# Reading a projection's 512 columns in pieces of 32: another order for TensorE's moving operand and its sums

## The chip, the core and the metric

One core of a Trainium2 chip runs the whole program in one launch. The metric is the device time of that launch in microseconds (us); three runs of the kernel before gave 1434.5, 1430.88 and 1432.8 us, median 1432.8. The profile was taken on one further execution.

## The reference, cut to what matters

One pre-norm residual layer on x (1 x 256 x 2048, float32), then a final RMSNorm. The combined input projection is the larger part of the work:

```python
h = _rms_norm(x, norm_g)
u = jnp.einsum('bsd,dn->bsn', h, w_in)            # 256 x 2048 times 2048 x 22672
a_in, b_in, b_gate, c_qkv, c_f, c_gate, d_in, d_gate, m_logit = _split(u, IN_SIZES)
# four mixers: gated short convolution, RWKV-7 recurrence, forgetting attention, causal pooling
proj = jnp.einsum('bskc,kcd->bskd', ys, w_branch)  # four times 256 x 1024 times 1024 x 2048
gates = jax.nn.sigmoid(m_logit.reshape(bsz, s, N_BRANCH, d) + b_merge)
merged = jnp.sum(gates * proj, axis=2)
return x + jnp.einsum('bsd,de->bse', merged, w_out)  # 256 x 2048 times 2048 x 2048
```

## The kernel before, in words

The 256 tokens are two row blocks of 128. Every large projection is a *chunk* of 512 output columns (`chunk`): its weights come from HBM two rows-of-128 at a time (512 KB in `raw`, three buffers, on SP's queue), and each 128 x 512 tile is split into two fp32r parts, a high one by ScalarE (`wh`, L267, six buffers) and a low one by VectorE (`wl`, L268, six buffers). The activations are split once into high and low parts (`xh`, `xl` for the input projection; `yah` to `ydl` for the branches; `mh`, `ml` for the output). `products` (L236 to L242) then issues three matmuls for each tile and row block: high x high (L240), high x low (L241), low x high (L242). In each, the activations are the stationary operand (128 x 128, loaded into the array by a weight load of its own, PEld), and the weights' part is the moving operand: its 512 columns are streamed, and 512 sums of each of the 128 rows are added into one PSUM tile `psm` (128 x 512 f32). A chunk of the input or output projection has 16 tiles, so 96 such matmuls; one of the branch projections has 8, so 48.

Two chunks are only 328 columns wide (`b_inputs`, half 1). The last chunk of the output projection puts all its split weights into the space of earlier tiles (`keep`) and runs row block 0 first, then row block 1 from the same parts; no weight is split in that second pass.

The order is fixed before the run: a scheduler places the instructions of each engine by the priorities of `level`. The weights' split has the first claim, then the RWKV block, then attention, then the rest. In the first 740 us the projections of the mixers are interleaved on PE with the many small matmuls of RWKV (the solver of L489 and L491 is a chain on VectorE) and of attention; from there on come the pooling branch, then 16 pairs of a gate chunk and a branch chunk, and the output projection, almost all of it chunks.

Where tiles lie: in the built program every tile that a chunk's matmul reads (`wh`, `wl`, `xh`, `xl`, `yah` to `ydl`, `yb`, `yc`, `ml1`) starts at an address, in bytes of its partition, that leaves 96 when divided by 512. 512 bytes are 128 columns of float32, and 128 bytes are one piece of 32 columns.

Of the kernel before, what the change touches and what calls it, by code (L numbers as in the profile page):

```python
# [9 lines left out]
F32 = mybir.dt.float32  # L10
F32R = mybir.dt.float32r
I32 = mybir.dt.int32
AF = mybir.ActivationFunctionType
# [4 lines left out]
P = 128  # L18
T = 256
NB = 2  # L20
D = 2048
W = 1024
CH = 512
HALF = 512
KG = 2
# [69 lines left out]
def kernel(  # L95
# [29 lines left out]
    sc = nc.scalar  # L125
# [6 lines left out]
    w_br_v = [w_branch[0, n].rearrange("(k p) n -> p k n", p=P) for n in range(4)]  # L132


    pers = ctx.enter_context(tc.tile_pool(name="pers", bufs=1))
    wpool = ctx.enter_context(tc.tile_pool(name="wpool", bufs=1))
    bc_pool = ctx.enter_context(tc.tile_pool(name="bc", bufs=2))
    ynat = ctx.enter_context(tc.tile_pool(name="ynat", bufs=1))
    wk = ctx.enter_context(tc.tile_pool(name="wk", bufs=1))
    ps_main = ctx.enter_context(tc.tile_pool(name="ps_main", bufs=3, space=PSUM))  # L140
# [2 lines left out]
    def psum_ex(tag, shape=(P, 512)):  # L143
        return ps_ex.tile(list(shape), F32, name="ps_" + tag, tag=tag, bufs=1 if tag == "z" else 2)
# [7 lines left out]
    @contextmanager  # L152
    def level(n):
        own, tc.cur_priority = tc.cur_priority, at[n]
        yield
        at[n], tc.cur_priority = tc.cur_priority, own


    rstd = pers.tile([P, NB], F32, name="rstd")
    nrstd8 = pers.tile([P, NB], F32, name="nrstd8")  # L160
    ngT = pers.tile([P, D // P], F32, name="ngT")
    ones1 = pers.tile([P, 1], F32, name="ones1")
    cq = pers.tile([P, NB, 16], F32, name="cq")
    fss = pers.tile([P, NB, 4], F32, name="fss")
    frs = pers.tile([P, NB], F32, name="frs")
    fa = pers.tile([P, NB, 16], F32, name="fa")
    xh = pers.tile([P, D // P, T], F32R, name="xh")
    xl = pers.tile([P, D // P, T], F32R, name="xl")
    cst = pers.tile([P, N_CONST], F32, name="cst")

    def load_constants(lo, hi):
        nc.sync.dma_start(out=cst[:, lo:hi], in_=consts[:, lo:hi])

    def K(name):
        lo, hi = _COFF[name]
        return cst[:, lo:hi]
# [3 lines left out]
    def bcast(src, n=CH, pool=bc_pool):  # L180

        t = pool.tile([P, n], F32, name="row", bufs=2)
        gp.dma_start(out=t, in_=src.unsqueeze(0).to_broadcast([P, n]))  # L183
        return t

    def mid(t):
        return t.unsqueeze(1).to_broadcast([P, NB, t.shape[-1]])
# [45 lines left out]
        v.tensor_scalar(out=nrstd8, in0=rstd, scalar1=-float(H) ** -0.5, scalar2=None, op0=ALU.mult)  # L233


    def products(ps, sth, stl, wh, wl, k, nk, n, b):  # L236
        cols = slice(b * P, (b + 1) * P)
        o = ps[b][:, :n]
        h, l = wh[:, :n], wl[:, :n]
        nc.tensor.matmul(o, lhsT=sth[:, k, cols], rhs=h, start=k == 0, stop=False)  # L240
        nc.tensor.matmul(o, lhsT=sth[:, k, cols], rhs=l, start=False, stop=False)  # L241
        nc.tensor.matmul(o, lhsT=stl[:, k, cols], rhs=h, start=False, stop=k == nk - 1)  # L242

    def new_ps():
        return [ps_main.tile([P, CH], F32, name="psm", tag="psm") for b in range(NB)]

    def chunk(ranges, nk, sth, stl, before=lambda g: None, keep=None):


        ps = new_ps()  # L250
        n = sum(r[2] for r in ranges)
        for g in range(nk // KG):
            wh, wl = [], []
            with level(WEIGHTS):
                before(g)
                raw = wpool.tile([P, KG, CH], F32, name="raw", bufs=3)
                at = 0
                for wv, c0, w in ranges:
                    nc.sync.dma_start(out=raw[:, :, at:at + w], in_=wv[:, g * KG:(g + 1) * KG, c0:c0 + w])
                    at += w  # L260
                for j in range(KG):
                    if keep:
                        h, l = keep(g * KG + j)
                    else:
                        h = wpool.tile([P, CH], F32R, name="wh", bufs=6)
                        l = wpool.tile([P, CH], F32R, name="wl", bufs=6)
                    sc.activation(out=h[:, :n], in_=raw[:, j, :n], func=AF.Copy)  # L267
                    v.tensor_tensor(out=l[:, :n], in0=raw[:, j, :n], in1=h[:, :n].bitcast(F32), op=ALU.subtract)  # L268
                    wh.append(h)
                    wl.append(l)  # L270
            for b in range(1 if keep else NB):
                for j in range(KG):
                    products(ps, sth, stl, wh[j], wl[j], g * KG + j, nk, n, b)
        if keep:
            for k in range(nk):
                products(ps, sth, stl, *keep(k), k, nk, n, 1)
        return ps

    def chunk_in(c0, n=CH, before=lambda g: None):
        return chunk([(w_in_v, c0, n)], D // P, xh, xl, before)  # L280
# [22 lines left out]
    def shift(dst, src, n):  # L303

        gp.memset(dst[0:n, 0, :], 0.0)
        gp.dma_start(out=dst[n:112 + n], in_=src[0:112])
        gp.dma_start(out=dst[112 + n:P], in_=src[112:P - n])
        gp.dma_start(out=dst[0:n, 1, :], in_=src[P - n:P, 0, :])
# [279 lines left out]
    def lora_and_forget(lu, cf):  # L588
        lp = wk.tile([P, NB, P], F32, name="qk", bufs=2)
        shift(lp, lu, 1)  # L590
        mub = bcast(rwkv_mu[0, 3072:3200], 128)
        v.tensor_tensor(out=lp, in0=lp, in1=lu, op=ALU.subtract)
        v.tensor_tensor(out=lp, in0=lp, in1=mid(mub), op=ALU.mult)
        v.tensor_tensor(out=lu, in0=lu, in1=lp, op=ALU.add)
        sc.activation(out=lu[:, :, 0:64], in_=lu[:, :, 0:64], func=AF.Tanh)
        tp = psum_ex("r")
        for b in range(NB):
            nc.tensor.transpose(tp[:, b * P:(b + 1) * P], lu[:, b, :], ident)

        for j, (own, other) in enumerate(((lo, hi), (hi, lo))):  # L600
            sc.activation(out=loraT[own, j, :], in_=tp[own, 0:T], func=AF.Copy)
            v.tensor_tensor(out=loraT[other, j, :], in0=tp[own, 0:T], in1=loraT[own, j, :].bitcast(F32),
                            op=ALU.subtract)


        bfb = bcast(fox_bf[0], 16)
        v.tensor_tensor(out=cf, in0=cf, in1=mid(bfb), op=ALU.add)
        sc.activation(out=fa, in_=cf, func=AF.Abs)
        sc.activation(out=fa, in_=fa, func=AF.Exp, scale=-1.0)
        sc.activation(out=fa, in_=fa, func=AF.Ln, bias=ones1)  # L610
        v.tensor_scalar(out=cf, in0=cf, scalar1=0.0, scalar2=None, op0=ALU.min)
        v.tensor_tensor(out=cf, in0=cf, in1=fa, op=ALU.subtract)
        tp = psum_ex("c")
        nc.tensor.matmul(tp[:, 0:16], lhsT=K("tri"), rhs=cf[:, 0, :], start=True, stop=True)
        v.tensor_copy(out=cq[:, 0, :], in_=tp[:, 0:16])
        tp = psum_ex("c")
        nc.tensor.matmul(tp[:, 0:16], lhsT=K("tri"), rhs=cf[:, 1, :], start=True, stop=False)
        nc.tensor.matmul(tp[:, 0:16], lhsT=K("ones"), rhs=cf[:, 0, :], start=False, stop=True)
        v.tensor_copy(out=cq[:, 1, :], in_=tp[:, 0:16])
# [165 lines left out]
    for hf in range(2):  # L785
# [4 lines left out]
        for g2 in range(2):  # L790
            g = hf * 2 + g2
# [25 lines left out]
    for dc in range(4):  # L817
        mg = wk.tile([P, NB, CH], F32, name="va")
        for n, nm in enumerate("abcd"):
            gt = gate_tile(dc, n)  # L820
            ps = chunk([(w_br_v[n], dc * CH, CH)], W // P, *yT[nm])
            for b in range(NB):
                if n == 0:
                    v.tensor_tensor(out=mg[:, b, :], in0=ps[b], in1=gt[:, b, :], op=ALU.mult)
                else:
                    v.tensor_tensor(out=gt[:, b, :], in0=ps[b], in1=gt[:, b, :], op=ALU.mult)
                    v.tensor_tensor(out=mg[:, b, :], in0=mg[:, b, :], in1=gt[:, b, :], op=ALU.add)
        split_T([mh[dc // 2], ml[dc // 2]], (dc % 2) * 4, mg, 4)
# [18 lines left out]
    def keep(k):  # L847
        if k < 8:
            return spare[0][:, k, :], spare[1][:, k, :]
        i = 2 + 2 * ((k - 8) // 4)  # L850
        return spare[i][:, k % 4, :], spare[i + 1][:, k % 4, :]

    for dc in range(4):
        fg = bcast(final_g[dc * CH:(dc + 1) * CH])
        ps = chunk([(w_out_v, dc * CH, CH)], D // P, Parts(mh), Parts(ml), keep=keep if dc == 3 else None)
# [53 lines left out]
```

## Time and profile before

| what | value |
|---|---|
| three runs | 1430.88, 1432.8, 1434.5 us |
| the profiled execution's own time | 1433.31 us |
| its span in the trace | 1431.5 us (1.8 us lie outside it) |
| mean granted TensorE clock | 0.994 |
| PE, PEld, DVE, ACT busy | 98%, 80%, 69%, 51% of the span |
| HBM read | 257.44 MB, 181 GB/s over the span |

A matmul's record is longer than the distance to the next one, since matmuls are pipelined: a busy PE says only that something was in the array. What one costs is read from the distance of starts. The chain of waits is followed back from the last instruction, and its shares tell which work the end depends on.

### The profile page before, as it was taken

Reading aid. Unit: us, or ns where it says so; the run is one execution under the profiler, and the core shown is the slowest. Engines: PE = TensorE matmul, PEld = TensorE weight load, DVE = VectorE, ACT = ScalarE, POOL = GpSimd, SP = SyncE. Lnnn points to the kernel's source line nnn. Section 1 sums busy time; section 2 is a strip of 40 time slices with the busy share of each in tenths; the row PEclk is TensorE's granted clock in tenths of the full one; section 3 lists DMA queues with packets and bytes.
Section 4 is the critical chain, followed back from the end, with each engine's and each line's share of the span. In section 5 each row is a group of like instructions: output and inputs, shape, how many; then the busy total and the mean of one; then the engine's idle time right before and its main releaser. Section 6 shows DMA issues by size and latency. Waiting matters only on the chain.

```text
span 1431.5 us, 19581 instructions
## 1 busy us (share of the span) xinstructions
PE 1398.8 (98%) x6913; PEld 1146.2 (80%) x6913; DVE 984.4 (69%) x1719; ACT 736.0 (51%) x1278; POOL 68.5 (5%) x135
## 2 busy tenths in 40 slices
PE   7999999999999899999999999999999999999997
PEld 5887778888887688887888888888888888888885
DVE  4558888589766889669957656666665666556654
ACT  6556644654455455554535544545545545444554
POOL 2110000001001000011000000000000000000000
PEclk9999999999999999999999999999999999999999
DMA  8776545456567646545655566666766666776664
GB/s 254 201 223 200 176 127 175 131 146 204 166 177 201 186 148 177 161 133 177 183 178 147 158 200 203 202 192 201 208 202 194 194 208 198 224 234 201 194 206 147
DMA packets 136626, 266.17 MB, mean 186 GB/s; under 512 B 11577, under 2 KB 15848, under 8 KB 136528
## 3 DMA queue, kind: packets, MB, share of 16 engines
q1 hardware_dynamic: 128768, 240.88, 55.5%
q0 software_dynamic: 7760, 24.04, 6.5%
q8 instruction: 54, 0.88, 0.3%
q14 instruction: 44, 0.36, 0.1%
HBM read 257.44 MB, written 2.10 MB: 181 GB/s over the span
## 4 chain that ended last, share of the span: by engine, by line
PE 67%; DVE 15%; DMA 11%; issue 4%; ACT 2%; POOL 1%; SPq 0%; ACTq 0%; DVEq 0%; POOLq 0%
PE psm L242 20%; PE psm L241 20%; PE psm L240 20%; DVE wl L268 6%; DMA raw<-in_w_in_dram 4%; DVE tm L489 2%; DMA cg<-pz 1%; DVE UQ L491 1%; DVE MT L482 1%; DMA raw<-in_w_out_dram 1%; DMA pv<-ur 1%; ACT wh L267 1%; PE ps_r L468 1%; PE ps_r L541 1%; DMA pv<-uv 1%
## 5 line engine op out<-in xcount | busy, mean ns | idle before, releaser
L267 ACT ACTIVATE wh<-raw 128x512 fp32r<-128x512 f32 (+1 forms) x896 | 545.7, 624 | 535.6 <-PE psm L242 361.3
L268 DVE TENSOR_TENSOR wl<-raw,wh 128x512 fp32r<-128x512 f32 (+1 forms) x896 | 596.5, 681 | 310.7 <-ACT wh L267 309.7
L241 PE MATMUL psm<-wl,xh 128*128 128x512 f32 (+1 forms) x1440 | 563.8, 393 | 7.0 <-DVE wl L268 6.6
L242 PE MATMUL psm<-wh,xl 128*128 128x512 f32 (+1 forms) x1440 | 562.1, 392 | 0.0
L240 PE MATMUL psm<-wh,xh 128*128 128x512 f32 (+1 forms) x1440 | 547.7, 393 | 4.0 <-ACT wh L267 3.4
L241 PEld LDWEIGHTS psm<-wl,xh 128*128 128x128 f32 x1440 | 271.3, 189 | 69.0 <-DVE wl L268 15.8
L240 PEld LDWEIGHTS psm<-wh,xh 128*128 128x128 f32 x1440 | 271.0, 189 | 62.6 <-ACT wh L267 7.2
L242 PEld LDWEIGHTS psm<-wh,xl 128*128 128x128 f32 x1440 | 271.6, 189 | 53.3 <-issue 1.2
L489 DVE TENSOR_TENSOR tm<-UQ,MT 128x16 f32<-128x16 f32 (+30 forms) x124 | 52.2, 421 | 2.0
L491 DVE TENSOR_REDUCE UQ<-tm 128x8 f32<-128x16 f32 (+30 forms) x124 | 36.0, 291 | 1.8
L183 POOL DMA_DIRECT2D row<-in_b_merge_dram x16 | 8.6, 539 | 502.6 <-DVE qa L742 431.8
L482 DVE STREAM_TRANSPOSE MT<-G 32x1024 f32<-32x1024 f32 x16 | 32.0, 2000 | 0.3
L742 DVE SCALAR_TENSOR_TENSOR qa<-psm,rstd,row 128x512 f32<-128x512 f32 x32 | 24.1, 752 | 9.7 <-PE psm L242 9.7
L659 ACT ACTIVATE pt<-pt,mx 128x128 f32<-128x128 f32 (+1 forms) x32 | 14.4, 450 | 23.7 <-DVE mx L657 23.6
L241 PE MATMUL psm<-wl,yah 128*128 128x512 f32 x64 | 24.9, 389 | 0.0
L242 PE MATMUL psm<-wh,yal 128*128 128x512 f32 x64 | 24.9, 389 | 0.0
L241 PE MATMUL psm<-wl,ybh 128*128 128x512 f32 x64 | 24.9, 389 | 0.0
L242 PE MATMUL psm<-wh,ybl 128*128 128x512 f32 x64 | 24.9, 389 | 0.0
L241 PE MATMUL psm<-wl,ych 128*128 128x512 f32 x64 | 24.9, 389 | 0.0
L242 PE MATMUL psm<-wh,ycl 128*128 128x512 f32 x64 | 24.9, 389 | 0.0
L241 PE MATMUL psm<-wl,ydh 128*128 128x512 f32 x64 | 24.9, 389 | 0.0
L242 PE MATMUL psm<-wh,ydl 128*128 128x512 f32 x64 | 24.9, 389 | 0.0
(378 smaller groups left out, 1365.7 us busy)
## 6 DMA issues: line engine op xcount, KB each, us to landing
raw<-in_w_in_dram SPq DMA_DIRECT2D x344, 512.0 KB, 4.1
raw<-in_w_branch_dram SPq DMA_DIRECT2D x64, 512.0 KB, 4.9
raw<-in_w_out_dram SPq DMA_DIRECT2D x32, 512.0 KB, 4.6
row<-in_b_merge_dram POOLq DMA_DIRECT2D x16, 256.0 KB, 4.3
raw<-in_w_in_dram SPq DMA_DIRECT2D x8, 328.0 KB, 4.0
raw<-in_w_in_dram SPq DMA_DIRECT2D x8, 312.0 KB, 3.6
x<-in_x_dram SPq DMA_DIRECT2D x4, 512.0 KB, 8.9
cg<-pz POOLq DMA_DIRECT2D x4, 448.0 KB, 4.8
```

The costliest lines, as they stand in the source:

```text
L240: nc.tensor.matmul(o, lhsT=sth[:, k, cols], rhs=h, start=k == 0, stop=False)
L241: nc.tensor.matmul(o, lhsT=sth[:, k, cols], rhs=l, start=False, stop=False)
L242: nc.tensor.matmul(o, lhsT=stl[:, k, cols], rhs=h, start=False, stop=k == nk - 1)
L267: sc.activation(out=h[:, :n], in_=raw[:, j, :n], func=AF.Copy)
L268: v.tensor_tensor(out=l[:, :n], in0=raw[:, j, :n], in1=h[:, :n].bitcast(F32), op=ALU.subtract)
L468: nc.tensor.matmul(gps[par][:, j * P:(j + 1) * P], lhsT=bk(rows, p, e), rhs=ar(rows, p, e), start=True, stop=True)
L482: v.transpose(out=MT[32 * q:32 * q + 32].rearrange("p t (r u) -> p t r u", u=NH), in_=src)
L489: v.tensor_tensor(out=tm[:, :, 0:n], in0=UQ[:, i:32, :].rearrange("p j c -> p c j"), in1=MT[:, i:32, i].unsqueeze(1).to_broadcast([P, 8, n ...
L491: v.tensor_reduce(out=UQ[:, i, :], in_=tm[:, :, 0:n], axis=AX.X, op=ALU.add)
L541: nc.tensor.matmul(ups[lo, hs], lhsT=UF[:, h, e, :], rhs=z[:, hs], start=True, stop=True)
L659: sc.activation(out=pt[:, s], in_=pt[:, s], func=AF.Exp, scale=-1.0, bias=mx[:, b:b + 1], accum_out=sm[:, b:b + 1])
L742: v.scalar_tensor_tensor(out=gt[:, b, :], in0=ps[b], scalar=rstd[:, b:b + 1], in1=bm, op0=ALU.mult, op1=ALU.add)
```

## The change

1. In a chunk of 512 columns, `by_place` replaces the three operands' plain 512 columns by a pattern of 16 pieces of 32 columns: first the fourth piece of each group of 128 columns (columns 96 to 127, 224 to 255, 352 to 383, 480 to 511), then the third piece of each group, the second and the first. The moving operand is read so, and the sums are written so: each column still lands in its own place.
2. The chunks of 328 columns, and all of the last output chunk (`plain=True`), stay as they are.
3. Small tiles (`rstd`, `cq` and others) go from the pool that is allocated first to one of their own behind the weights' tiles, and `ones1` gets 16 columns instead of one. With that the stationary tiles start at an address that leaves 128 when divided by 512, and `wh` and `wl` at one that leaves 256.

```diff
+    small = ctx.enter_context(tc.tile_pool(name="small", bufs=1))
...
-    ones1 = pers.tile([P, 1], F32, name="ones1")
+    ones1 = small.tile([P, 16], F32, name="ones1")
...
-    def products(ps, sth, stl, wh, wl, k, nk, n, b):
+    def by_place(t):
+
+        return bass.AP(tensor=t.tensor, offset=t.offset + 96, ap=[t.ap[0], (-32, 4), (P, 4), (1, 32)])
+
+    def products(ps, sth, stl, wh, wl, k, nk, n, b, plain=False):
         cols = slice(b * P, (b + 1) * P)
-        o = ps[b][:, :n]
-        h, l = wh[:, :n], wl[:, :n]
+        o, h, l = ps[b][:, :n], wh[:, :n], wl[:, :n]
+        if n == CH and not plain:
+            o, h, l = by_place(o), by_place(h), by_place(l)
         nc.tensor.matmul(o, lhsT=sth[:, k, cols], rhs=h, start=k == 0, stop=False)
...
-                    products(ps, sth, stl, wh[j], wl[j], g * KG + j, nk, n, b)
+                    products(ps, sth, stl, wh[j], wl[j], g * KG + j, nk, n, b, plain=keep is not None)
...
-                products(ps, sth, stl, *keep(k), k, nk, n, 1)
+                products(ps, sth, stl, *keep(k), k, nk, n, 1, plain=True)
```

The instructions of all five engines stand in the same order before and after; only line numbers, buffer numbers, the 16 columns of one memset and the shapes differ. On PE, where the first gate chunk ends (`xh`, `xl`) and the first branch chunk begins (`yah`, `yal`), there stands before (the last size is that of the sums):

```order
L240 MATMUL psm_7757<-wh_7918,xh_84 128x512
L241 MATMUL psm_7757<-wl_7919,xh_84 128x512
L242 MATMUL psm_7757<-wh_7918,xl_85 128x512
L240 MATMUL psm_7937<-wh_7941,yah_6808 128x512
L241 MATMUL psm_7937<-wl_7942,yah_6808 128x512
L242 MATMUL psm_7937<-wh_7941,yal_6809 128x512
```

And after, at the same place of PE:

```order
L248 MATMUL psm_7760<-wh_7921,xh_79 128x4x4x32
L249 MATMUL psm_7760<-wl_7922,xh_79 128x4x4x32
L250 MATMUL psm_7760<-wh_7921,xl_80 128x4x4x32
L248 MATMUL psm_7940<-wh_7944,yah_6811 128x4x4x32
L249 MATMUL psm_7940<-wl_7945,yah_6811 128x4x4x32
L250 MATMUL psm_7940<-wh_7944,yal_6812 128x4x4x32
```

Nothing moved; the pattern of the sums, and with it that of the moving operand, has become 4 x 4 x 32. Where PE goes from the third output chunk to the last, whose parts lie in the old places of `xh`, `xl` and others, the program after has these rows:

```order
L248 MATMUL psm_12644<-wh_12805,yc_7752 128x4x4x32
L249 MATMUL psm_12644<-wl_12806,yc_7752 128x4x4x32
L250 MATMUL psm_12644<-wh_12805,ml1_7754 128x4x4x32
L248 MATMUL psm_12831<-xh_79,yb_7751 128x512
L249 MATMUL psm_12831<-xl_80,yb_7751 128x512
L250 MATMUL psm_12831<-xh_79,ya_7753 128x512
```

The pattern ends with the third output chunk; the last one is read plainly, as before. So 5,184 of the kernel's chunk matmuls are patterned (43 whole chunks of the input projection x 96, 16 branch chunks x 48, three output chunks x 96), and 288 stay plain (192 of 328 columns, 96 of the last chunk). Seven matmuls at the start of a chunk gain a wait on an earlier matmul of PE itself and five of PE's other instructions lose one; seven of VectorE's instructions that read `psm` name PE as well in their wait.

## Rows read from the trace of the kernel before

**Rows 1.** The page's first section: busy time, share of the span, instructions.
```profile
PE 1398.8 (98%) x6913; PEld 1146.2 (80%) x6913; DVE 984.4 (69%) x1719; ACT 736.0 (51%) x1278; POOL 68.5 (5%) x135
```

**Rows 2.** Chain that ended last, by line: 0 to 740 us, then 740 to 1431.5.
```profile
by line: DVE wl L268 11.0%; PE psm L241 9.7%; PE psm L242 9.7%; PE psm L240 9.6%; issue 8.3%; DMA raw<-in_w_in_dram 8.2%; DVE tm L489 4.0%; DMA cg<-pz 2.7%; DVE UQ L491 2.5%; DVE MT L482 2.2%; DMA pv<-ur 2.0%; ACT wh L267 1.8%; PE ps_r L468
...
by line: PE psm L242 30.9%; PE psm L240 30.8%; PE psm L241 30.8%; DMA raw<-in_w_out_dram 2.3%; PE ps_r L768 0.8%; PE ps_z L768 0.8%; PE ps_c L806 0.5%; DVE xl L268 0.4%; DVE wl L268 0.3%; PE ps_c L800 0.3%; ACT xh L267 0.2%; PE ps_z L558 0.
```

**Rows 3.** PE in order of time: start us, us, engine line op names shapes.
```profile
830.90 0.39 PE L241 MATMUL psm<-wl,yah 128*128 128x512 f32 x1
...
928.82 0.39 PE L241 MATMUL psm<-wl,ydh 128*128 128x512 f32 x1
...
1050.12 0.39 PE L241 MATMUL psm<-wl,xh 128*128 128x512 f32 x1
1050.35 0.39 PE L242 MATMUL psm<-wh,xl 128*128 128x512 f32 x1
1050.58 0.39 PE L240 MATMUL psm<-wh,xh 128*128 128x512 f32 x1
```

**Rows 4.** PE in the 328-column chunks, in order of time.
```profile
84.52 0.31 PE L242 MATMUL psm<-wh,xl 128*128 128x328 f32 x1
84.67 0.31 PE L240 MATMUL psm<-wh,xh 128*128 128x328 f32 x1
...
85.72 0.31 PE L242 MATMUL psm<-wh,xl 128*128 128x328 f32 x1
```

**Rows 5.** Weight loads (PEld), in order of time, at two of these places.
```profile
84.52 0.19 PEld L240 LDWEIGHTS psm<-wh,xh 128*128 128x128 f32 x1
...
1050.13 0.19 PEld L242 LDWEIGHTS psm<-wh,xl 128*128 128x128 f32 x1
1050.35 0.19 PEld L240 LDWEIGHTS psm<-wh,xh 128*128 128x128 f32 x1
```

**Rows 6.** Stretches 148 to 156 us (columns as in rows 8); PE's matmuls there.
```profile
148.00:152.00 4.00, 2.10 (x8) 0.97 (x7) 3.94 (x6) 3.18 (x5) 0.54 (x1) 1.00 0.54 166
152.00:156.00 4.00, 3.83 (x10) 3.01 (x11) 4.00 (x7) 1.26 (x2) 0.00 (x0) 0.57 0.46 135
...
152.68 0.63 PE L241 MATMUL psm<-wl,xh 128*128 128x512 f32 x1
...
155.24 0.62 PE L241 MATMUL psm<-wl,xh 128*128 128x512 f32 x1
```

**Rows 7.** Two runs of plain f32 matmuls in order of time; groups: mean ns.
```profile
797.56 1.89 PE L806 MATMUL ps_c<-qk,sg 128*128 128x256 f32 x8
...
237.45 1.19 PE L507 MATMUL ps_r<-X,G 32*32 32x32 f32 x32 [0.26 <-DVE X L501]
...
L806 PE MATMUL ps_c<-qk,sg 128*128 128x256 f32 x32 | 8.1, 385 | 0.0
L507 PE MATMUL ps_r<-X,G 32*32 32x32 f32 x128 | 4.8, 192 | 0.4 <-DVE X L501 0.3
```

**Rows 8.** Stretches: PE, PEld, DVE, ACT, POOL busy us (x), PEclk, DMA share, GB/s.
```profile
300.00:400.00 100.00, 99.32 (x563) 81.48 (x563) 84.40 (x180) 48.74 (x92) 6.75 (x15) 1.00 0.56 166
925.00:1025.00 100.00, 100.00 (x447) 82.81 (x446) 60.38 (x91) 50.31 (x79) 1.61 (x3) 1.00 0.67 199
```

**Rows 9.** Who waited for whom: 0 to 740 us, then 740 on, then PE alone.
```profile
ACT wh L267 <- DMA raw<-in_w_in_dram: 102.7, 60, 4.7
DVE wl L268 <- ACT wh L267: 100.1, 89, 3.5
ACT wh L267 <- PE psm L242: 93.4, 71, 4.4
...
ACT wh L267 <- PE psm L242: 267.9, 209, 3.0
...
PE psm L241 <- DVE wl L268: 6.6, 13, 1.0
```

**Rows 10.** 825 to 1425 us: splitting operations (mean ns), DMA issues (us to landing).
```profile
L268 DVE TENSOR_TENSOR wl<-raw,wh 128x512 fp32r<-128x512 f32 x416 | 283.4, 691 | 195.1 <-ACT wh L267 195.0
L267 ACT ACTIVATE wh<-raw 128x512 fp32r<-128x512 f32 x416 | 262.3, 632 | 280.7 <-PE psm L242 249.2 <-DMA raw<-in_w_in_dram 7.8 <-DVE wl L268 5.9
...
raw<-in_w_branch_dram SPq DMA_DIRECT2D x61, 512.0 KB, 4.9
```

More of the change, by code (lines that the diff above doesn't have):

```diff
@@ L156, in level @@
         at[n], tc.cur_priority = tc.cur_priority, own
-    rstd = pers.tile([P, NB], F32, name="rstd")
-    nrstd8 = pers.tile([P, NB], F32, name="nrstd8")
-    ngT = pers.tile([P, D // P], F32, name="ngT")
-    ones1 = pers.tile([P, 1], F32, name="ones1")
[L163 to L166, printed above, removed]
     xh = pers.tile([P, D // P, T], F32R, name="xh")
@@ L169 @@
     cst = pers.tile([P, N_CONST], F32, name="cst")
+    fa = pers.tile([P, NB, 16], F32, name="fa")
+    rstd = small.tile([P, NB], F32, name="rstd")
+    nrstd8 = small.tile([P, NB], F32, name="nrstd8")
+    ngT = small.tile([P, D // P], F32, name="ngT")
+    ones1 = small.tile([P, 16], F32, name="ones1")
+    cq = small.tile([P, NB, 16], F32, name="cq")
+    fss = small.tile([P, NB, 4], F32, name="fss")
+    frs = small.tile([P, NB], F32, name="frs")
     def load_constants(lo, hi):
@@ L609, in lora_and_forget @@
         sc.activation(out=fa, in_=fa, func=AF.Exp, scale=-1.0)
-        sc.activation(out=fa, in_=fa, func=AF.Ln, bias=ones1)
+        sc.activation(out=fa, in_=fa, func=AF.Ln, bias=ones1[:, 0:1])
         v.tensor_scalar(out=cf, in0=cf, scalar1=0.0, scalar2=None, op0=ALU.min)
```

## The prediction

> **What bounds the kernel now.** I began with the busy shares [rows 1]: PE 98%, VectorE 69%, ScalarE 51%. A busy PE proves little, so I next followed the chain that ended last, cut at 740 us [rows 2]. From 740 us to the end the three chunk matmuls (L240 to L242) hold 30.9 + 30.8 + 30.8 = 92.5% of the chain: 0.925 x 691.5 = 639.6 us. Before 740 us they hold only 9.7 + 9.7 + 9.6 = 29.0%, 214.6 us; the rest is VectorE, DMA and small work. So the kernel has two halves: the second is PE's own pace, the first is a mixed chain in which PE is one of several.
>
> What is that pace? The order in time shows the first L241 of one branch chunk at 830.90 us and that of the fourth at 928.82 [rows 3]. By the code 432 chunk matmuls lie between them (three branch chunks of 48, three gate chunks of 96): 97.92 / 432 = 226.7 ns each, and the neighbours at 1050 us have the same distance. The 512 columns at one per cycle of the 2.4 GHz level take 213.3 ns. So 13.3 ns come on top.
>
> In the chunks of 328 columns eight distances take 85.72 - 84.52 = 1.20 us, 150.0 ns each [rows 4]. 328 / 2.4 is 136.7 ns: again 13.3 ns on top. The extra is therefore a price per matmul, not per column. Every matmul has a weight load of its own, and that starts together with the matmul before it (1050.13 beside 1050.12) and lasts 0.19 us [rows 5]: it reads the next stationary tile while the columns stream.
>
> Two stretches tell whether the price belongs to the load as such. From 152 to 156 us the granted clock is 0.57, most of it at the 1.2 GHz level, after 4 us in which PE was busy for 2.10; six distances there take 155.24 - 152.68 = 2.56 us, 426.7 ns each [rows 6], which is 512 / 1.2 with nothing on top. And the plain f32 matmuls of 256 columns at L806 start every (1890 - 385) / 7 = 215 ns [rows 7], two cycles per column (213.3) and about 2 ns. Both have a weight load for each matmul. Where the moving operand is read at half the rate, the 13.3 ns are gone. That looks like two reads that get in each other's way, the moving one and the load beside it, and less like a fixed hand-over.
>
> **The change part by part.** No instruction is added, removed or moved on any engine, and no DMA: the queues of SP and POOL are as they were. What there is to price is the new pattern, the addresses, and a few waits.
>
> *The pattern with the addresses.* Before, a matmul goes through all four pieces of 128 bytes in 512 over and over, 13.3 ns for each, so that whatever piece the load is reading, the stream comes upon it within 53.3 ns. After, it stays on one piece in 512 for 4 x 32 columns, 53.3 ns, and the new starts put it on another piece (remainders 128, 0, 384, 256 in turn) than the stationary tile's (128, 256, 384, 0 in its own order). If the reads collide by such pieces and the load goes through them in one direction, the stream can now keep clear of it. The trace shows neither the pieces nor the load's direction; I bound the result. At the one end all 13.3 ns go; at the other nothing does. I take 10.7 ns, which leaves 216 ns a matmul: the L806 distance, the nearest row in which a full-length stream runs beside a load without the extra [rows 7].
>
> *The price of a piece.* Sixteen runs of 32 columns take the place of one run of 512, in the read and in the write of the sums. No row shows a matmul with a broken pattern. From below: the jump is free. From above: each run costs as much as a small matmul of its own; the 32-column ones of L507 start every (1190 - 192) / 31 = 32 ns against 26.7 ns for 32 columns at two cycles, 5.5 ns too much, and 16 of those are 88 ns a matmul. I take nothing, since 32 columns in a row are 128 bytes without a gap and a start of an instruction is far more than a step of an address.
>
> *ScalarE, VectorE and DMA at new addresses.* Their operations keep shape and order. Gain or loss: I take nothing; where they wait on PE, a few ns are covered, and in the first half a loss of 1% of the 11.0 + 8.2% that VectorE's split and the weights' DMA hold of the chain [rows 2] would be 1.4 us, a gain the same.
>
> *The waits.* Seven matmuls now wait for an earlier one of PE, five others no longer do. One such wait costs at most the part of a record that overlaps the next, 0.39 - 0.227 = 0.16 us [rows 3]: 1.1 us if none of it were hidden. I take nothing. VectorE's seven wait for sums that PE must have finished anyway. More idle PE in the first half could bring more stretches at 1.2 GHz like that at 152 us [rows 6], where six matmuls lost 6 x 0.2 = 1.2 us; a few of them are within the range.
>
> *The sum.* The second half has 639.6 us / 226.7 ns = 2821 chunk matmuls on the chain, of which 96 stay plain: 2725 x 10.7 ns = 29.2 us. Is something else next there? ScalarE waits 267.9 us for PE to free its buffers after 740 us [rows 9], VectorE is busy 60.38 us in 100 against 84.40 in the first half [rows 8], and the weights' feed has room: a buffer of `raw` is held for a landing of 4.9 us, two splits of 0.632 us and one of 0.691 us behind, about 6.9 us, and with three of them one is ready every 2.3 us [rows 10], where PE will take one every 12 x 0.216 = 2.59 us (now 2.72). So all of it is kept.
>
> The first half has 214.6 / 0.2267 = 947 matmuls on the chain, 10.1 us at 10.7 ns. Here others follow closely: ScalarE waits 102.7 us for weights and only 93.4 us for PE, and PE has already come to a `wl` that wasn't ready 13 times [rows 9]. When PE is faster, the chain passes to VectorE and the DMAs at more places. I keep two thirds, 6.8 us.
>
> Together 36.0 us. The profiled execution took 1433.3 us (its span of 1431.5 and 1.8 outside), so 1397.3; it lay 0.5 us above the median of the three runs. Forecast: 1397 us.
>
> The range of this case: all 13.3 ns on all 3672 matmuls of the chain give 48.8 us, 1384; half of the extra, 6.7 ns, in the second half alone gives 18.3 us, 1415. The chain is inferred and may have a near rival in the first half; with 10.7 ns on all 5,184 patterned matmuls it would be 55.5 us, 1378.
>
> **The rivals.**
>
> *The 13.3 ns are a hand-over inside PE* and no order of reading touches them. For it: they are the same at 328 and 512 columns [rows 3, 4]. Against it: they are gone where the stream is slow though the loads are not fewer [rows 6, 7]; but a hand-over could hide there too, if the reading side has slack. The time would be 1433 plus or minus 2 us: the change doesn't do what it could. "TensorE: Matmul & The Clock Gate" of the Trainium skill, Part 2 (what happens when you issue a matmul), says that loading the next tile's weights doesn't steal read bandwidth from the running matmul, since there are two read ports. By that rule this rival holds and the sum is nil; the trace doesn't agree with it well, for the reason just given, but no row here shows two reads collide.
>
> *Broken patterns are slower.* The mechanism is a lost array cycle or more at each of the 16 runs, in the stream or at the sums. From 13.3 / 16 = 0.83 ns a run (two cycles at 2.4 GHz) it takes more than a full removal of the extra gives, and decides the sign. With one cycle (0.42 ns, 6.7 ns a matmul) and none of the extra removed, 2725 x 6.7 = 18 us come in the second half and, with two thirds of 947, 4 us in the first: 1455. With two cycles it is 1478. For it: the trace has no broken pattern that runs at full pace. Against: nothing but the length of the runs. "PSUM — Partial Sum Buffer" of the Trainium skill, Specifications (TRN2), says that any non-contiguous pattern there slows matmuls significantly; by it this rival would be the likeliest. No run here shows it.
>
> *The gain is eaten by the feed.* The matmuls get faster and PE then waits for `wl`, `wh` or weights in the second half as in the first. With a ready buffer only every 2.65 us, 216 ns would turn into 221 and 2725 x 5.9 ns = 16 us with nothing in the first half: 1417. Against it stand the 2.3 us worked out above.
>
> **How the numbers follow.** The forecast has 0.62 (range 1384 to 1415), the feed 0.09, the hand-over 0.13, the broken pattern 0.16. A measurement of this kernel can tell about 0.3%, 4.3 us, from no change. Faster: 0.62 + 0.09 = 0.71; within 0.3%: 0.13; slower: 0.16. The 8-in-10 range runs from 1378 over the feed to the hand-over's 1435; outside it lie the broken pattern and a small rest below.
>
> **What would show it.** Right: in the second half the first L241 (L249 after) of the first branch chunk and that of the fourth lie 432 x 0.216 = 93.3 us apart instead of 97.9; the 328-column chunks keep 150 ns unless the new addresses alone matter; ScalarE still waits for PE after 740 us; the busy share of VectorE there rises to about 63%; the chain before 740 us has a smaller share of L248 to L250 than 29%. Wrong: a distance of 226.7 ns (the hand-over) or above (the pattern), or 216 ns with gaps on PE behind `wl` (the feed). A second half that keeps its length with a shorter distance would break my reading of the chain.

## The result and the profile after

The changed kernel takes 1452.5 us (median of four runs, 1452.34 to 1454.63), the kernel before on the same chip 1433.05 us: a ratio of 1.0141, 95% interval 1.0123 to 1.0158. It is slower, by 19.5 us, where 1397 us were forecast and 1378 to 1435 given as the range. The time falls beside the 1455 us of the second rival, broken patterns; the experiments show that its mechanism is not the cause.

The page's busy times come first, the answer to [rows 1]: PE gained 23.6 us at the same count, the weight loads nothing.

```profile
PE 1422.4 (98%) x6913; PEld 1145.9 (79%) x6913; DVE 987.9 (68%) x1719; ACT 738.3 (51%) x1278; POOL 68.5 (5%) x135
```

Next PE in order of time (start us, us, engine, line, operation, names, shapes) at the places of [rows 3]: two neighbours in a branch chunk, and the same line in the fourth branch chunk.

```profile
834.30 0.40 PE L249 MATMUL psm<-wl,yah 128*128 128x512 f32 x1
834.54 0.40 PE L250 MATMUL psm<-wh,yal 128*128 128x512 f32 x1
...
935.10 0.40 PE L249 MATMUL psm<-wl,ydh 128*128 128x512 f32 x1
```

935.10 - 834.30 = 100.80 us for 432 matmuls: 233.3 ns each, where there were 226.7 and 216 were forecast. Up to the first of these rows the kernel had lost 834.30 - 830.90 = 3.4 us; behind it, to the end of the spans of 1431.5 and 1450.6 us, 15.7 us more. So the loss comes where the chunk matmuls are the chain. It isn't in all of them: two places carry no pattern, a chunk of 328 columns and the last output chunk, and here are the first and the last row of a stretch of each:

```profile
88.30 0.31 PE L250 MATMUL psm<-wh,xl 128*128 128x328 f32 x1
91.94 0.31 PE L248 MATMUL psm<-wh,xh 128*128 128x328 f32 x1
...
1436.23 0.39 PE L248 MATMUL psm<-xh,yb 128*128 128x512 f32 x1
1442.12 0.39 PE L250 MATMUL psm<-ydh,ml 128*128 128x512 f32 x1
```

24 distances at 328 columns take 3.64 us, 151.7 ns each, where there were 150.0. 26 in the last output chunk, both of whose operands lie in tiles that moved together, take 5.89 us, 226.5 ns each, as before. The prediction had the 328-column chunks at 150 ns "unless the new addresses alone matter"; by that sign they do. The second stretch of [rows 8] in the same columns (PE, PEld, DVE, ACT, POOL busy us, PEclk, DMA share, GB/s) shows the loss again:

```profile
925.00:1025.00 100.00, 100.00 (x434) 80.51 (x434) 59.50 (x89) 48.90 (x76) 1.61 (x3) 1.00 0.65 194
```

There 434 matmuls ran in place of 447, at the same granted clock of 1.00, and VectorE and the DMAs did less, because PE asked for less. The chain by line, cut at 740 us as in [rows 2], and the waits of [rows 9] (who waited for whom: us in total, times, longest in us; the first from before 740 us, the second from behind it, the third from PE alone over the whole span):

```profile
by line: PE psm L249 11.2%; PE psm L248 11.2%; PE psm L250 11.1%; DVE wl L276 6.5%; issue 6.4%; DVE MT L490 3.0%; DMA raw<-in_w_in_dram 2.7%; DMA cg<-pz 2.7%; DVE tm L497 2.5%; PE ps_r L476 1.5%; DVE UQ L499 1.5%; DMA pv<-uv 1.0%; PE ps_r L
...
by line: PE psm L250 32.0%; PE psm L249 32.0%; PE psm L248 31.9%; PE ps_r L776 0.8%; PE ps_z L776 0.7%; PE ps_c L814 0.5%; PE ps_c L808 0.2%; PE ps_z L566 0.2%; PE ps_z L542 0.2%; PE ps_r L549 0.2%; PE ps_z L538 0.1%; PE ps_c L809 0.1%; ACT
```

```profile
ACT wh L275 <- DMA raw<-in_w_in_dram: 91.3, 46, 4.5
...
ACT wh L275 <- PE psm L250: 291.6, 220, 3.1
...
PE psm L249 <- DVE wl L276: 3.8, 6, 1.3
```

The chunk matmuls now hold 33.5% of the chain before 740 us (29.0% before) and 95.9% behind it (92.5%); ScalarE waits longer for PE (267.9 us became 291.6) and PE less for `wl`. No other engine or transfer waits in a way that would explain it: the matmul itself became slower. The experiments ask why.

### The profile page after: what moved, and what is told of

It is laid out like the page before. It is cut to its first block, busy times and chain, and to the rows that moved or that the text cites. A ratio compares the mean times of both kernels' runs of the same rounds, so it can differ in the third digit from the quotient of the medians.

```text
span 1450.6 us, 19583 instructions
## 1 busy us (share of the span) xinstructions
PE 1422.4 (98%) x6913; PEld 1145.9 (79%) x6913; DVE 987.9 (68%) x1719; ACT 738.3 (51%) x1278; POOL 68.5 (5%) x135
## 4 chain that ended last, share of the span: by engine, by line
PE 71%; DVE 10%; DMA 5%; issue 3%; ACT 1%; POOL 1%; ACTq 0%; DVEq 0%; POOLq 0%
PE psm L249 21%; PE psm L248 21%; PE psm L250 21%; DVE wl L276 3%; DVE MT L490 2%; DMA raw<-in_w_in_dram 1%; DMA cg<-pz 1%; DVE tm L497 1%; PE ps_r L476 1%; DVE UQ L499 1%; PE ps_r L549 1%; DMA pv<-uv 1%; PE ps_z L566 1%; PE ps_c L814 1%; DMA pv<-ur 0%
## 5 line engine op out<-in xcount | busy, mean ns | idle before, releaser
L250 PE MATMUL psm<-wh,xl 128*128 128x512 f32 (+1 forms) x1440 | 568.2, 396 | 0.0
L248 PE MATMUL psm<-wh,xh 128*128 128x512 f32 (+1 forms) x1440 | 553.8, 397 | 4.1 <-ACT wh L275 4.1
```

## The experiments

Two kinds of kernel ran. Five are the whole program with one edit, timed against the kernel before. Five leave the whole encoder out: they run stretches of 36 to 48 equal fp32r matmuls into one PSUM tile each, every stretch with a start of the stationary and of the moving tile (bytes past a multiple of 512) and an order of its own. Their total time says nothing of the program; the distance of starts within a stretch does, and the difference of two neighbouring rows' starts over the count gives it to within a ns, since the first matmuls of a stretch can differ from the rest. (96, 352) stands for a stationary tile at 96 and a moving one at 352.

### Order, addresses and runs in isolation

The list of stretches, in short:

```diff
+    ('base', 96, 96, 'plain', 'plain', 512, 128),
+    ('addr', 128, 256, 'plain', 'plain', 512, 128),
+    ('both', 128, 256, 'by32', 'by32', 512, 128),
+    ('back', 128, 256, 'back32', 'back32', 512, 128),   # 16 runs of 32, last run first
```

> A kernel of its own that leaves the whole encoder out: 22 stretches of 48 fp32r matmuls (two of bf16) into one PSUM tile each, one weight load per matmul, all operands in place from the start. Each stretch changes one thing: addresses, order of the columns in the read, in the write, length and direction of the runs, rows of the stationary tile, columns. Read is the distance of starts within a stretch. Plain is known from before and after: 226.7 ns (512 columns and 13.3 ns), and after's pattern with after's addresses 233.3 ns. Theory A (each of 16 runs costs one cycle of 0.417 ns and the 13.3 ns stay): 2 runs 227.5, 4 runs 228.3, 8 runs 230.0, 16 runs 233.3, 32 runs 240.0 ns, whatever the addresses or the direction; broken in the read alone or in the write alone, one of the two has 233.3 and the other 226.7, or both. Theory B (the order does remove most of the 13.3 ns, and a run costs about 1.1 ns, more than I allowed): 233.3 with after's addresses, but about 244 with the old addresses or equal starts, and 8 runs with after's addresses fall below 226.7 or near it. Theory C (nothing of the 13.3 ns comes from two reads, a hand-over): 64 or 32 columns in the stationary tile keep 226.7. If two reads collide, the extra shrinks with the load: about 220 ns at 64 columns and 217 ns at 32.

PE in order of time, one row for a stretch:

```profile
25.94 11.05 PE L176 MATMUL pbase<-mv,st 128*128 128x512 f32 x48
36.83 11.32 PE L176 MATMUL paddr<-mv,st 128*128 128x512 f32 x48
47.98 11.37 PE L176 MATMUL pboth<-mv,st 128*128 128x512 f32 x48
59.19 11.37 PE L176 MATMUL poldaddr<-mv,st 128*128 128x512 f32 x48
70.40 11.36 PE L176 MATMUL preads<-mv,st 128*128 128x512 f32 x48
81.60 11.31 PE L176 MATMUL pwrites<-mv,st 128*128 128x512 f32 x48
92.74 11.32 PE L176 MATMUL phalves<-mv,st 128*128 128x512 f32 x48
...
126.46 11.06 PE L176 MATMUL pback<-mv,st 128*128 128x512 f32 x48
137.36 11.35 PE L176 MATMUL pquarters<-mv,st 128*128 128x512 f32 x48
...
243.57 10.53 PE L176 MATMUL pbfplain<-mb,sb 128*128 128x512 bf16 x48
253.94 10.52 PE L176 MATMUL pbfby<-mb,sb 128*128 128x512 bf16 x48
```

`base` runs at 226.9 ns, near the kernel before, `both` at 233.5, near the changed one: the effect is in the matmul alone. But `addr`, the plain order at the new starts, is at 232.3 already, and `back`, with as many broken runs as the change has, read and written, is at 227.1. So a run of 32 columns costs nothing by itself, which is against theory A, and the old starts with the new order (`oldaddr`) give 233.5 as well, which is against B. The pattern in the read alone (`reads`) takes 233.3 ns; in the write of the sums alone (`writes`) it takes 232.1, as the plain order there. What the order costs comes with the read. Theory C and the collision set against it both missed: 64 and 32 columns in the stationary tile take 229.8 and 231.7 ns, more than 226.7 and not less. In bf16 plain and pattern stand at about 216 both.

### The addresses alone, the order alone

```diff
-        if n == CH and not plain:
-            o, h, l = by_place(o), by_place(h), by_place(l)
```

> After with its addresses but every chunk read and written in plain order. Theory A and C: the addresses alone do nothing to a matmul, distance 226.7 ns, 1433 us, ratio 1.000 (within 0.3%). Theory B: the same, since a plain read meets every piece; 1433. A third view (the addresses have a price of their own on ScalarE, VectorE or the DMAs, and the pattern is not what costs): 1445 to 1453 us with the distance at 226.7 ns and more waits on wl and wh.

The changed kernel without the new order takes 1450.3 us, ratio 1.0134 (1.0119 to 1.0150). PE in order of time:

```profile
832.22 0.39 PE L247 MATMUL psm<-wl,yah 128*128 128x512 f32 x1
...
932.61 0.40 PE L247 MATMUL psm<-wl,ydh 128*128 128x512 f32 x1
```

100.39 us over 432 is 232.4 ns. The addresses by themselves make nearly the whole loss; the third view had the time, 1445 to 1453 us, but at an unchanged distance, and no theory had the distance. The other half, the new order in the kernel before with its tiles where they were:

> Before with its addresses (all starts 96 past a multiple of 512), with the patterned read and write of after. Theory A: distance 233.3 ns as in after, 1452 us, ratio 1.014. Theory B: the reads collide again, distance about 244 ns, second half 2725 x 17 ns = 46 us longer, about 1485 us.

```profile
837.75 0.40 PE L246 MATMUL psm<-wl,yah 128*128 128x512 f32 x1
...
939.99 0.40 PE L246 MATMUL psm<-wl,ydh 128*128 128x512 f32 x1
```

1466.6 us, ratio 1.0252 (1.0235 to 1.0269), 236.7 ns a matmul, between theory A's 233.3 and theory B's 244. The order costs more with the old starts than with the new ones, so the new starts do fit the new order in a sense; but each of the two leaves the place at which the kernel before stood.

### Which starts are quiet

The moving tile's start is swept in steps of 32 bytes with the stationary one at 96, all in plain order.

```diff
+    ('mc', 96, 64, 'plain', ...), ('md', 96, 96, ...), ('me', 96, 128, ...), ('mf', 96, 160, ...),
```

> A kernel of its own without the encoder, as the first: 38 stretches of 40 fp32r matmuls. In sixteen the moving operand starts at 0, 32, ... 480 past a multiple of 512 with the stationary one at 96, in eight the stationary one at 0, 64, ... 448 with the moving one at 96, all in plain order. Seen so far: 226.7 ns at (96, 96), 226.9 at (96, 352), a mean of 232.6 without a fixed step at (128, 256). Theory D (the distance depends on how the two starts stand to each other modulo 256 bytes: 0 is quiet, 128 is not): 226.7 at moving 96 and 352, 232 to 233 at moving 224 and 480, and the same values again wherever the difference is the same with the stationary start moved. Theory E (a start's own address decides, 96 being a good one): the moving sweep and the stationary sweep do not agree on equal differences. Theory F (the higher address bits decide, the real kernel steps its stationary tile by 1024 bytes and not by 512): the stretches with a step of 1024 differ from those of 512, patterned at (96, 96) 236 instead of 233.3. Fewer columns (448, 384, 328) at (96, 96): 13.3 ns on top of columns / 2.4 each time, 200.0, 173.3 and 150.0.

```profile
53.29 9.23 PE L192 MATMUL pmd<-mv,st 128*128 128x512 f32 x40
62.36 9.50 PE L192 MATMUL pme<-mv,st 128*128 128x512 f32 x40
...
127.56 9.26 PE L192 MATMUL pml<-mv,st 128*128 128x512 f32 x40
136.65 9.50 PE L192 MATMUL pmm<-mv,st 128*128 128x512 f32 x40
```

(62.36 - 53.29) / 40 = 226.8 ns at 96, and 227.3 at 352; two starts between (160 and 416) give 229.0, the other twelve 233.0 to 234.3. Eight stretches with other stationary starts, none of them equal to the moving one modulo 256, lie at 233.3 to 234.3, within 0.5 ns of the moving sweep at the same differences. Theory D stands: in plain order a fp32r matmul is quiet where both tiles start at the same remainder of 256 bytes. Before the change all of them did; the change set them 128 apart. With the stationary tiles 1024 bytes apart, as in the program, the pattern took 236.5 ns at (96, 96) and 233.5 at (128, 256), near the two values of the program. At (96, 96) with 512 bytes between them it had been 233.5, so for the pattern, as theory F has it, more than the remainder counts. One expectation missed: with 448 columns 203.0 ns were measured in place of 200.0 (384 and 328 columns gave 173.3 and 149.0), so the extra is not quite the same at every width.

In the program, with an unused tile of 384 bytes so that `wh` and `wl` start at the remainder of `xh` and `xl`, in plain order; the branches' tiles (`yah` and the like) then stand 128 off:

```diff
+    gap = pers.tile([P, 96], F32, name="gap")
+    gp.memset(gap, 0.0)
```

> The program with after's addresses and plain order, and one more change: a tile of 384 bytes ahead of the weights' buffers, so that wh and wl start 128 past a multiple of 512, as xh and xl do; the branches' tiles then start at 0, so their chunks have a difference of 128. Theory D: chunks with xh and xl are back at 226.7 ns, branch and output chunks (1,152 matmuls, difference 128) near 232.6: 1432 + 1152 x 5.9 ns = 1437 to 1439 us. Theory E (96 is a good address): all chunks near 232 to 233, about 1450 us. If ScalarE, VectorE or the DMAs made the loss of the second experiment: 1450 with 226.7 ns.

The first rows of a branch chunk, of the gate chunks behind it and of the next branch chunk:

```profile
828.14 0.41 PE L248 MATMUL psm<-wh,yah 128*128 128x512 f32 x1
...
839.30 0.39 PE L248 MATMUL psm<-wh,xh 128*128 128x512 f32 x1
...
861.07 0.41 PE L248 MATMUL psm<-wh,ybh 128*128 128x512 f32 x1
```

48 matmuls 128 bytes off take 11.16 us, 232.5 ns each; 96 with equal starts 21.77 us, 226.8 ns. One program holds both speeds, chunk by chunk, as the starts say. Its time is 1439.6 us, ratio 1.0044 (1.0029 to 1.0060): with 1152 matmuls off, 1152 x 5.7 ns = 6.6 us, and 7.2 were measured.

### Sixteen broken runs without the loss

```diff
-        ... offset=t.offset + 96, ap=[t.ap[0], (-32, 4), (P, 4), (1, 32)])
+        ... offset=t.offset + 480, ap=[t.ap[0], (-32, 16), (1, 32)])
```

> After with its addresses and its number of runs (16 of 32 columns, read and written), but in the order 480 to 511, 448 to 479, and so on down to 0 to 31. If a broken run costs a cycle each (Theory A, which the first experiment speaks against): 233.3 ns or more, 1452 us. If runs are free and only the order and the addresses set the distance: 226.7 ns as in the same stretch of the first experiment, about 1432 us.

```profile
833.57 0.39 PE L249 MATMUL psm<-wl,yah 128*128 128x512 f32 x1
...
931.49 0.39 PE L249 MATMUL psm<-wl,ydh 128*128 128x512 f32 x1
```

226.7 ns, and 1431.1 us, ratio 1.0001 (0.9985 to 1.0016). The same instructions at the changed addresses, each with 16 runs of 32 columns in its read and in its write, cost nothing when the runs go backwards through the tile. A backwards walk has a quiet difference too, 128 bytes instead of 0 (in the sweep above 226.8 at (128, 0), 232.0 and 232.3 at equal starts). What hurts is the order in which the pieces are read and not their number. The change's order stays on one piece in 512 bytes for 128 columns; that this is the harmful part of it is not shown, since one that alternates between two of the four pieces took 236.7 ns and about 240 in the next run.

### The search for a place below 226.7 ns

The pattern was then read at all sixteen moving starts, and the load made smaller:

```diff
+    ('qb', 96, 128, 'plain', 'plain', 512, 32, 128), ('hb', 96, 128, 'plain', 'plain', 512, 64, 128),
+    ('be', 128, 128, 'by32', ...), ('bf', 128, 160, ...), ('bg', 128, 192, ...),
```

> A kernel of its own without the encoder: 42 stretches of 36 fp32r matmuls. Stationary tiles of 32 and of 64 columns instead of 128 with the start of the moving operand swept over 256 bytes in steps of 32; after's pattern with the stationary start at 128 and the moving start swept over 512 bytes; plain order with the start shifted by 8 to 56 bytes from the quiet place; and a read of all even pieces of 32 before all odd ones. Theory G (13.3 ns are a floor that every fp32r matmul pays, and collisions with the weight load come on top, 0 at the quiet start): no stretch has a mean below 226.6 ns, whatever the start, the order or the load's columns; the sweep with 32 columns reaches 226.7 at some start. Theory H (also the 13.3 ns at the quiet start are reads that collide, in proportion to the load): at 32 columns the sweep reaches 217 to 220 at some start, at 64 about 220, and some start of the pattern goes below 226.6. For the pattern: 233.3 or 236.6 at all 16 starts if no start suits it; 226.7 at some if only its start was chosen badly. Shift from the quiet place: already away from 226.7 at 8 or 16 bytes if lines of the memory matter, still there if only pieces of 128 bytes do.

The pattern gave 233.3 to 239.4 ns, with one exception at 160, about 216. I took that for the place that the change had been after.

```profile
200.34 7.95 PE L197 MATMUL pbf<-mb,sb 128*128 128x512 bf16 x36
207.94 8.76 PE L197 MATMUL pbg<-mv,st 128*128 128x512 f32 x36
```

The type at the row's end says what it was: a stretch named `bf` had been given the bf16 tiles. I read it only after the next run. Smaller loads did not help: with 64 stationary columns 226.9 to 232.8 ns, with 32 columns 230.6 to 238.9. Equal starts were not even the quiet ones there (230.3 and 231.7 ns), so the rule found above is one for loads of 128 columns. That the 13.3 ns shrink with the load, the first half of theory H, falls. Theory G is right that no fp32r stretch lies below 226.6 ns, and wrong that 32 columns reach 226.7 somewhere. In plain order a start 8 bytes off the quiet place is at 233.1 ns already. The program with `wh` and `wl` at 160 (the changed kernel with two more unused tiles):

```diff
+    gap = pers.tile([P, 104], F32, name="gap")
+    gap2 = small.tile([P, 24], F32, name="gap2")
```

> After with its pattern, and two unused tiles (416 and 96 bytes) that put wh and wl at 160 past a multiple of 512 instead of 256, while the stationary tiles stay at 128. In the sweep just run the pattern had 215.85 ns at that one start of sixteen and 233.3 to 240.0 at the others. Theory H (the 13.3 ns are reads that collide, and the pattern keeps clear of them from the right start; the change's step was right and its start wrong): distance 215.9 ns in the chunks of the real program too, and by the chain of the kernel before 2725 x 10.8 ns = 29 us in the second half and about 7 us in the first: about 1396 us, ratio 0.975. If the address were good only in the small kernel (Theory G): 226.7 ns or more, 1431 us or more. If the feed takes over: 216 ns with idle PE behind wl, about 1415 us.

1470.6 us, ratio 1.0268 (1.0247 to 1.0290), 233.3 ns in some chunks and 240.0 in others. What was left of theory H rested on the misread row and is gone. The two speeds stand in matmuls of the same tiles: of `wh` and `wl` with `xh` and `xl`, 18 distances from 825.10 us take 240.0 ns each, and 33 from 832.64 us take 233.3. So for the pattern the remainders of the starts do not fix the distance. Around that start, in steps of 8 bytes:

> A kernel of its own without the encoder: 36 stretches of 36 fp32r matmuls. The pattern with stationary start 128 and moving start 128 to 208 in steps of 8; with other stationary starts (0, 96, 384) and the moving one 32 past each; with 64 and 32 stationary columns; broken in the read alone and in the write alone; and the pieces in upward order with the moving start swept over 512 bytes. If the difference of the starts decides: 215.9 ns at (0, 32), (96, 128), (384, 416). If the width of the good place is a line or two: 215.9 only at 152 to 168; if it is a good part of a piece: over 40 bytes or more. Read alone 215.9 ns, write alone as plain at that start, 231 to 233 ns. If the load goes through its columns in one direction only, the upward order has no start at 215.9; if it reads them all at once or in either direction, it has one too.

```profile
25.07 8.56 PE L191 MATMUL pfa<-mv,st 128*128 128x512 f32 x36
33.47 9.54 PE L191 MATMUL pfb<-mv,st 128*128 128x512 f32 x36
42.85 8.57 PE L191 MATMUL pfc<-mv,st 128*128 128x512 f32 x36
```

At 128 and 144 the pattern takes 233.3 and 233.6 ns, at 136 260.6: eight bytes off a multiple of 16 cost 27 ns here. In plain order they do nothing of the kind (232.5 to 235.0 ns at four such starts in the sweep of the loads). The same pieces in rising order give 233.3 to 239.4 at all sixteen starts. The last run asks what the 13.3 ns are. One stretch reads the same column 512 times, one loads one column 128 times, and eight stay within one piece of 32 columns:

```diff
+    "one": (0, [(0, 512)]), "stay32": (0, [(0, 16), (1, 32)]),
```

> A kernel of its own without the encoder: 31 stretches of 36 matmuls, plain order unless said. The 215.85 ns that the sweep showed at one start of the pattern came from a stretch that the kernel ran in bf16 because of its name; so no fp32r stretch has yet been below 226.6 ns. What is the floor of 13.3 ns made of? fp32r: the moving operand reads one and the same column 512 times, or one piece of 32 columns 16 times (eight places of it); the stationary operand is one column 128 times, or every second column (1024 bytes instead of 512); 64 partitions instead of 128. bf16: plain with eight starts over 256 bytes, and the pattern with six starts. Theory G (a price that every fp32r matmul pays whatever is read): 226.7 with one column read by either side, and nothing below. Theory I (it is the load's read that holds up the stream): 215 to 217 with one column as the load, about 240 with the doubled load. Theory J (it is the stream's own reading): 215 to 217 with one column as the stream, the load changes nothing. bf16: 215.85 at all starts if half the bytes leave room for every collision; a spread of some ns over the starts if not.

```profile
23.47 8.32 PE L192 MATMUL pbase<-mv,st 128*128 128x512 f32 x36
31.63 7.93 PE L192 MATMUL poneread<-mv,st 128*128 128x512 f32 x36
39.40 7.93 PE L192 MATMUL pbothone<-mv,st 128*128 128x512 f32 x36
47.17 8.50 PE L192 MATMUL ploadone<-mv,st 128*128 128x512 f32 x36
55.51 8.50 PE L192 MATMUL ploadonefar<-mv,st 128*128 128x512 f32 x36
```

A stream that re-reads one column runs at 215.8 ns with its normal load beside it. A load that reads only one column does not help (231.7), and one spread over twice the bytes takes 233.1, so theory I falls. Staying in one piece, the extreme of what the change does, is worse than walking: 235.6 to 239.7. Theory J, that the 13.3 ns are the stream's own price of reading fp32r columns, has its first half, the 215.8 ns; its second, that the load changes nothing, does not hold, since the load of one column moved the distance from 226.7 to 231.7. Every stretch had a load for each matmul, so whether the 13.3 ns would stand without one is not shown. Of the fp32r stretches that read 512 different columns, none came under 226.6 ns.

## Why the prediction was wrong

**What bounds the kernel: right.** The loss per matmul, put on the chain as I put the gain, gives the loss of the kernel. With all of the second half's 2725 and two thirds of the first half's 947, 3356 matmuls: 5.7 ns more is 19.1 us (the addresses alone measured 19.7), 6.6 ns is 22.1 us (the change, 19.5), 10 ns is 33.6 us (the order alone, 36.1). That is within 3 us each time.

**The 13.3 ns as a price of reading: right in kind.** They go away when the stream re-reads one column, so they aren't a fixed hand-over inside PE. What part the load has in them is open.

**"I take 10.7 ns, which leaves 216 ns a matmul": the step that failed.** I read the extra as a collision of which an order that stays on one piece could keep clear, and took its size from L806. Those rows read at half the rate: the 16 matmuls written there stand as 32 in the trace, each with two cycles per column. No row of the kernel before has a full-rate fp32r stream without the extra. The runs put the extra at 13.3 ns at the best place found and at more elsewhere, and the kernel before stood at that place. The change left it twice: the starts 128 bytes apart cost 5.7 ns (1450.3 us alone), and the order costs 6.6 to 13.3 at every start tried. Together they cost 6.6, not 5.7 + 10. My bounds were at fault too: at the one end all of it goes, at the other "nothing does". [Rows 3] showed one pair of starts only, so it could not tell a floor from an average, and the far end should have lain below nothing.

**The price of a piece at nothing: right,** though the time came out beside the rival that denied it. One cycle at each of 16 runs is 6.7 ns, and 6.6 were measured; the backwards runs show the agreement to be luck. "PSUM — Partial Sum Buffer" of the Trainium skill, Specifications (TRN2), which I had put beside that rival, has non-contiguous patterns slow a matmul significantly; the runs do not agree for runs of 32 columns (226.7 ns with and without in the program, 232.1 against 232.3 with the write of the sums alone broken, about 216 with and without in bf16).

**The hand-over rival** was right in that no order tried takes the 13.3 ns away, and wrong that addresses do not touch the matmul. The rule that I named with it, in "TensorE: Matmul & The Clock Gate" of the Trainium skill, Part 2, has the next load steal no read bandwidth. The bf16 stretches agree (215.8 to 216.1 ns at eight starts); in fp32r the distance depends on where the two tiles start relative to each other (226.7 against 233), which fits it badly.

**The other terms.** ScalarE, VectorE and the waits at nothing: right, as far as the busy times and the edit with backwards runs (ratio 1.0001) show it. The feed never came into play, since PE asked for less.

**What stays open.** Why the load's place matters while its width hardly does, and why the order costs what it does, I could not settle. The remainders of the starts describe the plain order with loads of 128 columns; for the pattern they do not suffice, and no run shows the inside. No version beat the kernel before.

## What to carry to other kernels

Where fp32r matmuls bound a kernel, compare the starts of the stationary and the moving tiles: in plain order an equal remainder of 256 bytes was worth 6 ns of 233 here, and a small tile declared ahead of them can undo it, so measure the distance of starts in the trace after each change of layout. Before an extra is priced as removable, run the bare matmul at several starts: one place tells no floor from an average, and a row at half the rate tells nothing of what is left at full rate. A time that agrees with a rival is no proof of its mechanism; read the whole row, type and shape included, before building on it.

## What the runs showed that was not expected

- fp32r matmuls of 512 columns with loads of 128 depend on how the starts of their two operands stand to each other: 226.7 to 235.0 ns in plain order, least at an equal remainder of 256 bytes. At 328 columns it is 150.0 against 151.7 in the program.
- The bf16 stretches do not: 215.8 to 216.1 ns at eight starts, and 215.8 with the pattern at six.
- The pattern with its runs 8 bytes off a multiple of 16 took 260.0 to 266.4 ns.
- Re-reading one column brings fp32r to 215.8 ns, the pace of bf16.
